# A tenth raw weight buffer, dead activation tiles as weight buffers in the last product, and one activation combination formed sooner

## The chip, the cores and the metric

The kernel runs on one core of a Trainium2 chip. The time is device microseconds (us) of one execution, from several timed runs; the profile is one further execution, taken by the hardware profiler. The core has five engines with a stream of instructions each: TensorE (PE in the profile: matmuls; PEld is its weight load), VectorE (DVE), ScalarE (ACT), GpSimd (POOL) and SyncE (SP). An engine takes its own instructions strictly in order; between engines there are semaphores. SP and POOL are used here mostly to issue transfers (DMAs) from the chip's HBM into the on-chip memory.

## The reference

The network has two layers and a final RMS norm, on 512 tokens of 1024 features, in float32.

```python
for l in range(DEPTH):                       # DEPTH = 2
    x = x + 0.5 * swiglu(rms_norm(x, ffn1_norm[l]), ffn1_w_in[l], ffn1_w_out[l])
    x = x + mixer(rms_norm(x, mix_norm[l]), mix_w_in[l], mix_gate_bias[l], na_rpb[l],
                  na_w_out[l], f_w_out[l], mix_w_o[l])
    x = x + 0.5 * swiglu(rms_norm(x, ffn2_norm[l]), ffn2_w_in[l], ffn2_w_out[l])
return rms_norm(x, final_norm)

def swiglu(x, w_in, w_out):                  # w_in 1024 x 5632, w_out 2816 x 1024
    g, u = jnp.split(x @ w_in, 2, axis=-1)
    return (jax.nn.silu(g) * u) @ w_out

# mixer: z = h @ w_in; neighbourhood attention on q, k, v; a 2-D DFT on uf; gates ga, gf
return (sigmoid(ga + gate_bias[0]) * y_na + sigmoid(gf + gate_bias[1]) * y_f) @ w_o
```

The mixer's `w_in` has 4096 columns, of which the last 2048 make the two gates. `w_o` is 1024 x 1024.

## The kernel before

**Arithmetic.** Each float32 operand of a large product is split into a high and a low part (ACT rounds the high part, DVE subtracts it from the value), and a product is three matmuls: high by high, high by low, low by high (lines 539, 540 and 542). Each large product is moreover formed by Strassen's scheme of seven block products instead of eight, numbered 1 to 7 by `m` in the code. A block product needs a combination of blocks of activations (`t5`, `t6`, `t7` for three of them in an FFN) and a combination of blocks of weights. The PSUM pairs A, B and C hold the seven results.

**Weights.** They are streamed from HBM in granules of 128 x 1024 float32 (512 KB), called `raw` when they land. For every granule there is a `Raw` object. Its `load` takes a buffer and issues the transfer on SP (line 155). Where `plus` is given, POOL then issues a second transfer that adds another granule onto the buffer as it lands, an accumulating DMA (line 165). DVE does other such sums itself (line 182). `Item.prep` then splits the granule: `whi` on ACT (line 210) and `wlo` on DVE (line 213). In the gates and in the output product one more accumulating DMA follows, from `Item.prep`, on POOL:

```python
            if self.then:
                G.dma_start(out=t, in_=wst[GRAN_AT[self.then]][:, 0:n], accum_op=ALU.add)   # line 215
```

The granule d that product 6 has just split gets block b added in place (`then=b.key`) and is split a second time for product 3. A block has two granules, so product 3 waits for two of these adds. They are issued after the splits for product 6, and POOL issues them in the place that the program gives them.

**Order.** One list of items runs through the whole program. `Stream.prep` issues loads ahead of the split, up to `depth` items beyond the one being split; `depth` is FETCH = 8 throughout. A load waits on SP until its buffer is free. In the FFNs, the gates and the mixer's output product the buffers are a ring of nine (`ffn_raw`, line 2022); in the rest of the mixer another ring (`mix_raw`). Since `load` issues the line 165 add right behind the SP load in the program, how far ahead the loads are issued also sets where those adds stand in POOL's program, against the line 215 adds.

**Stages.** Per layer: FFN1 (blocks of 2816 hidden columns, then the output product), mixer (attention, DFT, two gate blocks of seven products each, output product `w_o` on the pairs wA, wB, wC), FFN2, whose first block (`first_block`) runs while the norm of its input is still being finished. There DVE forms `t6` by the generator `combine`: a sum `xr` (line 651), a high part on ACT (line 656), and a low part `t6l` (line 658), behind product 5 in the code. The last output product of the network (`late`) runs with nothing behind it but the final norm.

Of the kernel before, what the change touches and what calls it, by code (L numbers as in the profile page):

```python
# [9 lines left out]
F32 = mybir.dt.float32  # L10
# [8 lines left out]
P = 128  # L19
# [15 lines left out]
FETCH = 8  # L35
# [63 lines left out]
def encoder_kernel(  # L99
# [15 lines left out]
    def nm(s):  # L115
        uid[0] += 1
        return f"{s}_{uid[0]}"

    def slot(dt=F32, s="k", shape=(4, 256)):
        return kp.tile([P, *shape], dt, tag="k", name=nm(s), bufs=23)  # L120
# [219 lines left out]
    ws = Stream()  # L340
    raw_pool = [None]
# [15 lines left out]
    def small(s, n=8):  # L357
        return sp.tile([P, 8], F32, tag=s, name=nm(s), bufs=2)[:, 0:n]
# [304 lines left out]
    def stage_ffn(norm, nxt, late):  # L663
# [45 lines left out]
        def combine(m):  # L709
            for _ in steps_of(m):  # L710
                pass
# [165 lines left out]
        def first_block():  # L877

            f0 = 2

            def snap_T(ps):
                t = slot(F32, "sn", (2, 256))
                S.activation(t, ps.rearrange("p (m t) -> p m t", m=2), AF.Copy)
                return t

            def less_T(ps, t):
                V.tensor_tensor(t, ps.rearrange("p (m t) -> p m t", m=2), t, ALU.subtract)

            pa, ha = pair("A"), bank("hA")
            product(pa, acts[1], K4, True)  # L890
            combine(5)
            s1 = snap(pa)
            if len(norm.due) == 2:
                norm.quad(*norm.due.pop(0))
            product_T(ha, acts[1], True)
            h1 = snap_T(ha)
            pb, hb = pair("B"), bank("hB")
            product(pb, acts[5], K4, True)
            combine(6)
            sb = snap(pb)  # L900
            norm.settle()
            product_T(hb, acts[5], True)
            hsb = snap_T(hb)
            norm.rstd()
            norm.spread(R)
            product(pa, acts[6], K4, False, again=True)
            s2 = snap(pa)
            combine(7)
            product_T(ha, acts[6], False)
            h2 = snap_T(ha)  # L910
            pc = pair("C")
            product(pc, acts[2], K4, True)
            less(pc, s1)
            combine(4)
            z1 = gate(s1, 0)
            product(pa, acts[7], K4, False, again=True)
            hc = bank("hC")
            product_T(hc, acts[2], True)
            less_T(hc, h1)
            r1 = half_gate(h1, 0)  # L920
            less(pa, sb)
            product_T(ha, acts[7], False)
            less_T(ha, hsb)
            product(pb, acts[3], K4, False, again=True)
            less(pb, s2)
            z2 = gate(s2, 1)
            times(z2, [sb[:, 0, :], sb[:, 1, :]], 1)
            product_T(hb, acts[3], False)
            less_T(hb, h2)
            r2 = half_gate(h2, 1)  # L930
            half_times(h2, r2, hsb, hsb, 1)
            z2 = words_apart(z2)
            product(pa, acts[4], K4, False, again=True)
            turned.append((turned_words(z2), 1, f0))
            times(z1, pa, 0)
            halves(z1, 0, f0)
            released(turned[-1][0])
            product_T(ha, acts[4], False)
            half_times(h1, r1, ha.rearrange("p (m t) -> p m t", m=2), h2, 0)
# [50 lines left out]

        if late or nxt.mix:
            tc.keep_in_program_order(S.activation(small("sq", 1), ones, AF.Sqrt))
        ps = {}
        for i, (m, c, _) in enumerate(steps):
            make(i)
# [135 lines left out]
    def stage_mixer(l, norm, nxt):  # L1131
# [783 lines left out]
        with tc.manual_schedule(engines={mybir.EngineType.DVE, mybir.EngineType.Activation}):  # L1915
            w = [ws.next(0), ws.next(0)]
            ws.prep(ws.pos + 1)
            ws.fetch(ws.prepped + 9)
            f_turn(0)
            h1 = high(t12, "t1")  # L1920
            acts[5] = low(h1, t12, "t1")
            for _ in fill(o, ns, 0, w):
                pass
            for z in B[1, 1]:
                V.tensor_tensor(t12, t12, z, ALU.add)
            h2 = high(t12, "t2")
            next(third)
            acts[6] = low(h2, t12, "t2")
            next(third)
# [89 lines left out]
    mix_pool = [None]  # L2019

    def ffn_raw(n):
        return scope_pool[0].tile([P, 1024], F32, tag="raw", name=nm("raw"), bufs=9)[:, 0:n]

    def mix_raw(n):
        return slot(F32, "raw", (1024,))

    scope_pool = [None]

    def swap_pools(kind, fetch=True):

        if scope[0]:
            scope[0].close()
        scope[0] = ExitStack()
        name = nm("stage")
        scope_pool[0] = scope[0].enter_context(tc.tile_pool(name=name, bufs=1, reuse_waits="tile"))
        if kind:
            mix_pool[0] = scope_pool[0]
            raw_pool[0] = mix_raw
        else:
            raw_pool[0] = ffn_raw  # L2040
        if fetch:
            ws.enter(ws.stage + 1)

# [207 lines left out]
```

## Time and profile before

| | |
|---|---|
| median of 3 runs | 1840.56 us (1840.37 to 1847.86) |
| the profiled execution's own time | 1838.69 us |
| its span, first to last instruction | 1836.9 us |
| mean granted TensorE clock | 0.999 |
| PE busy | 1824.8 us, 99% of the span |
| DVE busy | 1607.9 us, 88% |
| ACT busy | 1306.6 us, 71% |
| POOL busy | 179.2 us, 10% |
| transfers | 403.75 MB, mean 220 GB/s |

In the table of busy time, 99% for PE leaves little idle time to look for; the places where PE waits are in the view of waits. A row of that view reads: engine and line, what it waited for, microseconds in total, how many times, and the longest. In a timeline a row is start, duration, engine, line, operation, output<-inputs with shapes, count, and in square brackets the idle time of the engine before it with what released it. A row of the view of transfers tells the line of issue, the count, the size and the median us from issue to landing.

### The profile page before, as it was taken

What the parts mean: (1) busy time and instruction counts of PE and PEld (TensorE: products, weight loads), DVE (VectorE), ACT (ScalarE), POOL (GpSimd) and SP (SyncE); (2) the same over time, 40 slices, a digit from 0 to 9 for tenths busy, and PEclk for the clock granted to TensorE, in tenths of its full rate; (3) what the DMA queues carried; (4) which work ended last, traced back from release to release, by engine and by line L of the source; (5) the groups of instructions that cost most, each with busy time, mean ns of one, the idle gap of its engine ahead of it and who ended that gap; (6) DMA issues with size and microseconds to landing.
All of it is one profiled execution on the core that took longest, in us unless ns stands there. A gap on an engine that the chain in (4) does not pass through costs nothing.

```text
span 1836.9 us, 24500 instructions
## 1 busy us (share of the span) xinstructions
PE 1824.8 (99%) x8766; PEld 1509.6 (82%) x8766; DVE 1607.9 (88%) x1952; ACT 1306.6 (71%) x1771; POOL 179.2 (10%) x219
## 2 busy tenths in 40 slices
PE   9999999999999999999999999999999999999998
PEld 7888888887788888888888888888888788888886
DVE  7878899778889987889998888998789899887899
ACT  6777875767577776787666778766776776677865
POOL 0001011110111011001010100101001111100010
PEclk9999999999999999999999999999999999999999
DMA  9888798963997788879878887998649977988795
GB/s 303 222 236 224 187 277 267 227 175 112 276 240 186 170 228 234 217 199 281 249 188 215 232 217 196 263 305 184 177 135 262 234 184 184 236 214 223 199 290 143
DMA packets 206386, 403.75 MB, mean 220 GB/s; under 512 B 108732, under 2 KB 108892, under 8 KB 206264
## 3 DMA queue, kind: packets, MB, share of 16 engines
q1 hardware_dynamic: 176536, 300.52, 51.5%
q0 software_dynamic: 29296, 101.12, 30.2%
q8 instruction: 69, 1.13, 0.2%
q10 hardware_dynamic: 432, 0.55, 0.1%
q14 instruction: 53, 0.43, 0.1%
HBM read 370.67 MB, written 2.11 MB: 203 GB/s over the span
## 4 chain that ended last, share of the span: by engine, by line
PE 78%; DVE 7%; DMA 7%; issue 4%; ACT 3%; POOL 0%; SPq 0%; DVEq 0%; ACTq 0%; POOLq 0%
PE A L540 9%; PE A L542 9%; PE A L539 9%; DMA raw<-in_wst_dram 6%; PE o L542 6%; PE o L540 5%; PE o L539 5%; PE B L542 4%; PE B L540 4%; PE B L539 4%; DVE wlo L213 2%; PE ps L344 2%; PE C L542 2%; PE C L540 2%; PE C L539 2%
## 5 line engine op out<-in xcount | busy, mean ns | idle before, releaser
L213 DVE TENSOR_TENSOR wlo<-raw,whi 128x1024 fp32r<-128x1024 f32 (+1 forms) x534 | 632.0, 1193 | 164.6 <-ACT whi L210 163.0
L210 ACT ACTIVATE whi<-raw 128x1024 fp32r<-128x1024 f32 (+1 forms) x534 | 546.1, 1033 | 270.1 <-DVE raw L182 57.3
L165 POOL DMA_DIRECT2D raw<-in_wst_dram x170 | 148.7, 899 | 1301.9 <-DMA raw<-in_wst_dram 630.8
L182 DVE TENSOR_TENSOR raw<-raw,raw 128x1024 f32<-128x1024 f32 (+1 forms) x148 | 176.5, 1193 | 2.0
L540 PE MATMUL A<-whi,xl 128*128 128x512 f32 x400 | 155.8, 390 | 0.0
L539 PE MATMUL A<-whi,xh 128*128 128x512 f32 x400 | 155.8, 390 | 0.0
L394 ACT ACTIVATE at<-zt 128x1024 uint16<-128x1024 uint16 (+2 forms) x96 | 110.4, 1167 | 11.2 <-DMA zt<-zs 11.1
L205 ACT ACTIVATE whi<-raw 128x1024 fp32r<-128x1024 f32 (+1 forms) x83 | 85.7, 1037 | 43.4 <-PE A L540 13.3
L542 PE MATMUL A<-wlo,xh 128*128 128x512 f32 x400 | 115.1, 389 | 0.0
L206 DVE SCALAR_TENSOR_TENSOR wlo<-raw,whi 128x1024 fp32r<-128x1024 f32 (+1 forms) x83 | 98.7, 1195 | 11.5 <-ACT whi L205 11.5
L542 PEld LDWEIGHTS A<-wlo,xh 128*128 128x128 f32 x400 | 75.1, 188 | 15.5
L539 PEld LDWEIGHTS A<-whi,xh 128*128 128x128 f32 x400 | 75.1, 188 | 15.4
L540 PEld LDWEIGHTS A<-whi,xl 128*128 128x128 f32 x400 | 75.2, 188 | 15.4
L539 PE MATMUL B<-whi,xh 128*128 128x512 f32 x208 | 81.3, 391 | 0.8 <-ACT whi L210 0.8
L540 PE MATMUL B<-whi,xl 128*128 128x512 f32 x208 | 81.1, 390 | 0.0
L540 PE MATMUL C<-whi,xl 128*128 128x512 f32 x208 | 81.0, 390 | 0.0
L539 PE MATMUL C<-whi,xh 128*128 128x512 f32 x208 | 81.0, 390 | 0.0
L375 ACT ACTIVATE zs<-th 128x1024 uint16<-128x1024 uint16 x80 | 79.5, 1042 | 0.4 <-DVE th L801 0.4
L626 ACT ACTIVATE sn<-A 128x512 f32<-128x512 f32 x104 | 58.8, 586 | 27.3 <-PE A L542 27.2
L794 ACT ACTIVATE th<-sn,rh 128x512 f32<-128x512 f32 x80 | 54.9, 715 | 31.3 <-DVE sn L631 30.4
L542 PE MATMUL B<-wlo,xh 128*128 128x512 f32 x208 | 60.2, 391 | 0.2
L542 PE MATMUL C<-wlo,xh 128*128 128x512 f32 x208 | 60.1, 391 | 0.0
(451 smaller groups left out, 4624.2 us busy)
## 6 DMA issues: line engine op xcount, KB each, us to landing
raw<-in_wst_dram SPq DMA_DIRECT2D x468, 512.0 KB, 6.1
raw<-in_wst_dram POOLq DMA_DIRECT2D x180, 512.0 KB, 8.0
bm<-in_bias_dram SPq DMA_DIRECT2D x16, 512.0 KB, 5.5
raw<-in_wst_dram SPq DMA_DIRECT2D x30, 256.0 KB, 5.4
vs<-v SPq DMA_DIRECT2D x24, 128.0 KB, 5.4
x<-in_xin_dram SPq DMA_DIRECT2D x4, 512.0 KB, 10.2
raw<-in_wst_dram POOLq DMA_DIRECT2D x8, 256.0 KB, 8.2
dft<-in_dft_dram POOLq DMA_DIRECT2D x8, 256.0 KB, 6.8
```

Source lines behind the costliest of these rows:

```text
L165: G.dma_start(out=self.t, in_=wst[GRAN_AT[self.plus]][:, 0 : self.n], accum_op=ALU.add)
L182: V.tensor_tensor(self.raw.t, self.raw.t, self.add.t, ALU.add)
L205: S.activation(hi, t, AF.Copy, scale=-1.0)
L206: self.last = V.scalar_tensor_tensor(lo, t, -1.0, hi.bitcast(F32), ALU.mult, ALU.subtract)
L210: S.activation(hi[:, cs], t[:, cs], AF.Copy)
L213: self.last = V.tensor_tensor(lo[:, cs], t[:, cs], hi[:, cs].bitcast(F32), ALU.subtract)
L375: S.activation(s[:, h], words[:, h], AF.Copy)
L394: S.activation(to[:, w], t[:, w], AF.Copy)
L539: PE.matmul(ps, lh, rh, start=start, stop=False, skip_group_check=again)
L540: PE.matmul(ps, ll, rh, start=False, stop=False, skip_group_check=again)
L542: PE.matmul(ps, lh, rl, start=False, stop=stop, skip_group_check=again)
L626: last_snap[0] = S.activation(t[:, b, :], ps[b], AF.Copy)
```

## The change

Four edits.

1. The ring `ffn_raw` gets ten buffers instead of nine, and `depth` is FETCH + 1 = 9 wherever that ring is used (FFNs, gates, output product). At the start of the gates, `ws.fetch` goes to ten items instead of nine.
2. In the last FFN's output product the weights also go into the two buffers each of the tiles `xh` and `xl`, which no longer hold activations needed there: four further buffers of 1024 columns, then five from the ring. `depth` becomes 16.
3. In `first_block` (both FFN2s), the first step of combination 6 (`xr`, line 651) is taken by a hook after the first granule of product 5, and its other steps after the product.
4. `swap_pools` sets the depth back to FETCH in the parts of the mixer that use the other ring.

```diff
@@ first_block @@
-            product(pb, acts[5], K4, True)
-            combine(6)
+            six = steps_of(6)
+            product(pb, acts[5], K4, True, hook=lambda: next(six))
+            for _ in six:
+                pass
@@ stage_ffn, ahead of the output product @@
+        if late:
+            raw_pool[0] = late_raw
+            ws.depth = 16
@@ start of the gates @@
-            ws.fetch(ws.prepped + 9)
+            ws.fetch(ws.prepped + 10)
@@ the pools @@
-        return scope_pool[0].tile([P, 1024], F32, tag="raw", name=nm("raw"), bufs=9)[:, 0:n]
+        return scope_pool[0].tile([P, 1024], F32, tag="raw", name=nm("raw"), bufs=10)[:, 0:n]
+    spare = []
+
+    def late_raw(n):
+        if not spare:
+            for tag in ("xh", "xl"):
+                t = np_.tile([P, 2, 1024], F32, tag=tag, name=nm("raw"), bufs=2)
+                spare.extend(t[:, i, :] for i in range(2))
+            spare.extend([None] * 5)
+        t = spare.pop(0)
+        return ffn_raw(n) if t is None else t[:, 0:n]
@@ swap_pools @@
             raw_pool[0] = mix_raw
+            ws.depth = FETCH
         else:
             raw_pool[0] = ffn_raw
+            ws.depth = FETCH + 1
```

What this does to the order of instructions shows in three places.

The first is POOL at the first gate block of layer 0 (layer 1 is alike). `raw_4207` and `raw_4210` are the two granules of block d; their line 215 rows are the adds that product 3 waits for. The other rows are line 165 adds; `raw_4513` before and `raw_4497` after are the same granule, the first combined one of the second gate block. Before:

```order
L165 DMA raw_4207<-in_wst_dram 128x1024
L165 DMA raw_4210<-in_wst_dram 128x1024
L165 DMA raw_4279<-in_wst_dram 128x1024
L165 DMA raw_4282<-in_wst_dram 128x1024
L215 DMA raw_4207<-in_wst_dram 128x1024
L215 DMA raw_4210<-in_wst_dram 128x1024
L165 DMA raw_4513<-in_wst_dram 128x1024
L165 DMA raw_4556<-in_wst_dram 128x1024
```

After:

```order
L165 DMA raw_4207<-in_wst_dram 128x1024
L165 DMA raw_4210<-in_wst_dram 128x1024
L165 DMA raw_4275<-in_wst_dram 128x1024
L165 DMA raw_4282<-in_wst_dram 128x1024
L215 DMA raw_4207<-in_wst_dram 128x1024
L165 DMA raw_4497<-in_wst_dram 128x1024
L215 DMA raw_4210<-in_wst_dram 128x1024
L165 DMA raw_4516<-in_wst_dram 128x1024
```

The add for the next block now stands between the two line 215 adds.

The second is POOL at the mixer's output product of layer 0 (layer 1 is alike), where the line 215 rows belong to the output product's product 3 and the line 165 rows to FFN2 behind it. Before:

```order
L215 DMA raw_4880<-in_wst_dram 128x1024
L215 DMA raw_4901<-in_wst_dram 128x1024
L165 DMA raw_5264<-in_wst_dram 128x1024
L165 DMA raw_5288<-in_wst_dram 128x1024
L165 DMA raw_5342<-in_wst_dram 128x1024
```

After:

```order
L215 DMA raw_4864<-in_wst_dram 128x1024
L165 DMA raw_5260<-in_wst_dram 128x1024
L215 DMA raw_4883<-in_wst_dram 128x1024
L165 DMA raw_5267<-in_wst_dram 128x1024
L165 DMA raw_5291<-in_wst_dram 128x1024
```

Here too a line 165 add of the next stage comes between the two.

The third is DVE in FFN2's first block of layer 0 (layer 1 is alike): line 651 makes `xr`, line 658 `t6l`, lines 182 and 213 are weight sums and low parts, lines 365 to 367 small steps of the norm. Before:

```order
L182 TENSOR_TENSOR raw_5288<-raw_5288,raw_5223 128x1024
L367 SCALAR_TENSOR_TENSOR r_5644<-rt_5645,r_5644 128x4
L213 TENSOR_TENSOR wlo_5566<-raw_5264,whi_5565 128x1024
L365 TENSOR_TENSOR rt_5645<-r_5644 128x4
L651 TENSOR_TENSOR xr_5325<-xr_5490,xr_5325 128x1024
L366 SCALAR_TENSOR_TENSOR rt_5645<-rt_5645,ms_5641 128x4
L182 TENSOR_TENSOR raw_5342<-raw_5342,raw_5258 128x1024
L367 SCALAR_TENSOR_TENSOR r_5644<-rt_5645,r_5644 128x4
L658 TENSOR_TENSOR t6l_5584<-xr_5325,t6h_5583 128x1024
```

After:

```order
L651 TENSOR_TENSOR xr_5328<-xr_5493,xr_5328 128x1024
L367 SCALAR_TENSOR_TENSOR r_5644<-rt_5645,r_5644 128x4
L182 TENSOR_TENSOR raw_5267<-raw_5267,raw_5199 128x1024
L365 TENSOR_TENSOR rt_5645<-r_5644 128x4
L213 TENSOR_TENSOR wlo_5570<-raw_5260,whi_5569 128x1024
L366 SCALAR_TENSOR_TENSOR rt_5645<-rt_5645,ms_5641 128x4
L658 TENSOR_TENSOR t6l_5587<-xr_5328,t6h_5586 128x1024
```

The sum `xr` and the low part `t6l` each stand one large instruction earlier: two large ones (a line 182 and a line 213) stood between `xr`'s new place and its old one, and one line 182 sum that was ahead of `t6l` now comes behind it.

PE's order is the same before and after. SP issues the same loads, each about one granule earlier against the work.

## The prediction, made before the change was run

> **What bounds the kernel now.** I began with the page: busy time and the summary of the chain that ended last. Then I read PE's own waits, and a stretch in which nothing waits (the last row: window, length, busy time and count for PE, PEld, DVE, ACT and POOL, then the granted clock, the transfers' share and GB/s).
>
> ```profile
> PE 1824.8 (99%) x8766; PEld 1509.6 (82%) x8766; DVE 1607.9 (88%) x1952; ACT 1306.6 (71%) x1771; POOL 179.2 (10%) x219
> PE 78%; DVE 7%; DMA 7%; issue 4%; ACT 3%; POOL 0%; SPq 0%; DVEq 0%; ACTq 0%; POOLq 0%
> PE A L540 <- DVE t6l L658: 0.9, 2, 0.5
> PE B L539 <- ACT whi L210: 0.8, 1, 0.8
> PE o L542 <- DVE wlo L213: 0.2, 1, 0.2
> 500.00:550.00 50.00, 50.00 (x218) 40.42 (x218) 44.98 (x50) 36.10 (x38) 5.16 (x6) 1.00 0.92 238
> ```
>
> PE is busy for 1824.8 us, 12.1 short of the span of 1836.9 us. In the stretch from 500 to 550 us it does 218 matmuls without a gap, 0.229 us each, at a clock of 1.00; nothing can make these shorter here, since the change leaves PE's instructions and their order alone. So there are 12.1 us of idle PE time in all, and the three waits account for 1.9 us of them. A gain of over 0.5%, 9.2 us, isn't to be had. Losses have no such limit: PE has no slack to give, and any operand that comes later than now lengthens the run one for one. So the question is which operands come sooner and which come later.
>
> **The gains.** *Combination 6.* The row with `t6l` is the place that the third edit touches: PE wants it twice (once per FFN2) and waits 0.9 us in all, 0.5 at most.
>
> ```profile
> 614.69 1.22 DVE L182 TENSOR_TENSOR raw<-raw,raw 128x1024 f32<-128x1024 f32 x1
> ```
>
> In the changed order this large sum, 1.22 us, stands behind `t6l` and no longer ahead of it, which is more than either wait. So the waits go: 0.9 us (bounds nothing, if another operand is as late, and 2.4, the two sums). The sum that is moved back, and the low part that it feeds, are wanted by PE only a granule later.
>
> *Last output product.* Here the raw granules come late: ACT waits for them, and PE's weight load for what follows. The second part is for FFN1's output product of layer 1, which also gets one more buffer, the third for the rest of layer 1's gates.
>
> ```profile
> ACT whi L210 <- DMA raw<-in_wst_dram: 6.4, 4, 3.1
> PEld o L542 <- DVE wlo L213: 1.5, 3, 0.6
> PEld o L539 <- ACT whi L210: 0.4, 1, 0.4
> ...
> ACT whi L210 <- DMA raw<-in_wst_dram: 7.7, 5, 2.6
> PEld o L542 <- DVE wlo L213: 1.7, 4, 0.5
> ...
> PEld B L542 <- DVE wlo L213: 0.9, 2, 0.5
> ```
>
> (The views are the waits from 1765 to 1837 us, 1170 to 1225, and 1411 to 1460.) A weight load may wait in the shadow of a matmul still running, so its wait is the upper bound of PE's: 1.9 us for the last product, against 0.2 in PE's own list as the lower. With four more buffers and a depth of 16 its granules are asked for well ahead; I take 1.3 us, in the upper half, because the three waits there come one after another with nothing else late. For FFN1's product (0 to 1.7) one granule more of lead helps less against a queue already full: 0.5. For the gates (0 to 0.9): 0.5, as much from the PE delay told below as from the buffer. The four gains sum to 0.9 + 1.3 + 0.5 + 0.5 = 3.2 us.
>
> **The losses.** Ten buffers instead of nine let SP issue each load a granule sooner, and the line 165 add that belongs to a load moves up with it in POOL's program. At four places it moves between the two line 215 adds for which product 3 waits: the first gate block and the mixer's output product, in both layers. What an add costs that is queued behind another one, the trace shows at these very places. First POOL at the gates of layer 0, with its landing times (each of the three rows on transfers is the answer for one issue, in order: 483.87, 485.67, 487.41), then what waits:
>
> ```profile
> 483.87 0.85 POOL L215 DMA_DIRECT2D raw<-in_wst_dram  x1 [15.26 <-DVE wlo L213]
> 485.67 0.85 POOL L215 DMA_DIRECT2D raw<-in_wst_dram  x1 [0.95 <-DVE wlo L213]
> 487.41 0.86 POOL L165 DMA_DIRECT2D raw<-in_wst_dram  x1 [0.88 <-DMA raw<-in_wst_dram]
> 498.51 0.86 POOL L165 DMA_DIRECT2D raw<-in_wst_dram  x1 [10.24 <-DMA raw<-in_wst_dram]
> raw<-in_wst_dram POOLq DMA_DIRECT2D x1, 512.0 KB, 7.1
> raw<-in_wst_dram POOLq DMA_DIRECT2D x1, 512.0 KB, 11.1
> raw<-in_wst_dram POOLq DMA_DIRECT2D x1, 512.0 KB, 13.3
> 496.89 2.96 ACT L210 ACTIVATE whi<-raw 128x1024 fp32r<-128x1024 f32 x3 [3.79 <-DMA raw<-in_wst_dram]
> 498.00 0.50 PE L539 MATMUL B<-whi,xh 128*128 128x512 f32 x1 [0.78 <-ACT whi L210]
> ```
>
> The three are issued within 3.5 us and land at 491.0, 496.8 and 500.7: in the order of issue, the third 3.9 us behind the second. The second is the one that counts. ACT takes it up at 496.89, 0.1 us after it lands, and PE has already been waiting 0.78 us when it gets `whi`: slack zero. In the changed order this add is third, so it lands at about 500.7. POOL can issue it late by the wait of the add put ahead of it (0.88 us here) and 0.86 us for that issue, which still falls before the first one lands; the queue decides. Loss: **3.9 us**. Layer 1:
>
> ```profile
> 1397.20 0.85 POOL L215 DMA_DIRECT2D raw<-in_wst_dram  x1 [0.95 <-DVE wlo L213]
> 1399.99 0.86 POOL L165 DMA_DIRECT2D raw<-in_wst_dram  x1 [1.93 <-DMA raw<-in_wst_dram]
> raw<-in_wst_dram POOLq DMA_DIRECT2D x1, 512.0 KB, 10.2
> raw<-in_wst_dram POOLq DMA_DIRECT2D x1, 512.0 KB, 11.2
> 1407.49 2.96 ACT L210 ACTIVATE whi<-raw 128x1024 fp32r<-128x1024 f32 x3 [2.16 <-DMA raw<-in_wst_dram]
> 1408.60 0.19 PEld L539 LDWEIGHTS B<-whi,xh 128*128 128x128 f32 x1 [0.27 <-ACT whi L210]
> ```
>
> They land at 1407.4 and 1411.2; PE's weight load again waits already (0.27 us). Loss: **3.8 us**. For the output product, layer 0:
>
> ```profile
> 575.15 0.86 POOL L215 DMA_DIRECT2D raw<-in_wst_dram  x1 [20.91 <-ACT whi L210]
> 577.19 0.86 POOL L215 DMA_DIRECT2D raw<-in_wst_dram  x1 [1.18 <-DVE wlo L213]
> raw<-in_wst_dram POOLq DMA_DIRECT2D x1, 512.0 KB, 5.2
> raw<-in_wst_dram POOLq DMA_DIRECT2D x1, 512.0 KB, 8.3
> 585.60 1.06 ACT L210 ACTIVATE whi<-raw 128x1024 fp32r<-128x1024 f32 x1 [2.48 <-DMA raw<-in_wst_dram]
> 590.18 1.23 DVE L351 TENSOR_TENSOR m4l<-mq,m4h 128x1024 fp32r<-128x1024 f32 x1
> 591.83 0.39 PE L540 MATMUL wA<-whi,m4l 128*128 128x512 f32 x1
> ```
>
> Here the adds land at 580.4 and 585.5, 5.1 us apart. ACT takes the second up at 585.60, and the low part on DVE follows; behind that low part DVE's program has `mq`, then `m4l`, which ends at 591.41 and is read at 591.83. That is 0.4 us of slack; PE itself reads the granule's `whi` later than it is made, so the `m4l` chain binds. A third add in the queue puts the second 3.8 us later by the gate rows, 5.1 by the pair here; I take 3.8, as the third place in the queue is what was measured there. Loss: 3.8 - 0.4 = **3.4 us**. In layer 1 the same chain has 0.3 us of slack:
>
> ```profile
> 1501.37 1.23 DVE L351 TENSOR_TENSOR m4l<-mq,m4h 128x1024 fp32r<-128x1024 f32 x1
> 1502.92 0.39 PE L540 MATMUL wA<-whi,m4l 128*128 128x512 f32 x1
> ```
>
> Loss: **3.5 us**. The four sum to 3.9 + 3.8 + 3.4 + 3.5 = 14.6 us. Bounds for one place: nothing, if the queue lets the later add through unhindered, and 12.8 us, if POOL waits for the load of the add put ahead as it did at 498.51 (498.51 - 485.67), with the line 215 add behind it.
>
> The rest costs nothing that I can see. The load that the moved add needs is issued one granule sooner as well; elsewhere the earlier loads take SP and queue time that PE doesn't wait for. In the last product the extra buffers come free by PE's own reads of `xh` and `xl`.
>
> **A rule against the row.** The Trainium skill, "DMA: Bandwidth & Descriptors", section "Anatomy of one DMA — SWDGE (gpsimd) path", puts one GpSimd-issued DMA at a fixed 2.0 us plus bytes over 436 GB/s, most of the fixed part being completion latency; for 512 KB I estimate 1.2 us of movement, which is all that a queued DMA would add to the next. By that the four places would lose about 1.2, 1.2, 0.8 and 0.9, 4.1 us. The rows above have 3.8 to 5.1 us instead, while SP's queue is full too; I go by the rows.
>
> **The sum.** 14.6 - 3.2 = +11.4 us on the profiled execution's 1838.69 us: 1850.1. The median of the runs, 1840.56, is 1.9 us above that execution, so the runs should come to **1852.0 us**, 0.6% more than before. What can be told from no change is 0.5%, or 1831.4 to 1849.8 us.
>
> **The rivals.**
> *A. The moved adds are hidden.* POOL's transfers go through 16 engines side by side, and an add that is ready later might not hold up the next. Then only the gains stay: 1840.6 - 3.2 = 1837.4 us, no change by the bound. Against it: at the gates all three land in order, nearly evenly spaced, as in one queue. A cheap queued add belongs here too: a third of the spacing (1.3 us) at four places is 5.2 less 0.7 of slack, 4.5, and the time 1841.9. (The skill's figure would put it at about the same place: 4.1 - 3.2, so 1841.5.)
> *B. Only the gates pay.* At the output product the pair lands 5.2 and 8.3 us after issue, against 7.1 to 13.3 at the gates, so the queues are emptier there, and the add put between may land early enough. Then 7.7 - 3.2 = +4.5: 1845.1 us, no change by the bound. Against it: the second of that pair already lands 5.1 us behind the first.
> *C. POOL itself is blocked.* POOL waits in order for the load of the moved add, 10.24 us in one row above. If that happens at one of the four, with the line 215 add behind it, 12.8 us take the place of 3.8 there: 1852.0 + 9 = 1861.0. For it: the load comes through a queue whose transfers land late at the gates. Against it: the load is itself a granule earlier.
> *D. The gain is larger than PE's waits.* Only the 12.1 us of idle PE time could give it, and part of that is the start and the final norm. Faster by 0.5% would need nine of the twelve.
>
> **How the numbers follow.** I give the forecast 0.56, A 0.20, B 0.16, C 0.07, D 0.01. The forecast's own range is 1847 to 1857: with 2.6 us per place instead of 3.8 it is 4.8 less, with 5.1 it is 5.2 more. About four fifths of it lies above 1849.8, 0.46, which with C makes slower 0.53; same is 0.10 + 0.20 + 0.16 = 0.46; faster 0.01. For 8 in 10 the range reaches down to most of A and leaves the far end of C out: 1838 to 1857.
>
> **What would show it.** In the changed profile the waits of PE should have the row for `whi` behind product 3 of the gates at about 4 us, at both layers, and a wait of `wA` for `m4l` of 3 us or more at both output products. In POOL's timeline there, a line 165 add stands between the line 215 adds, and the second of these lands 3.8 us later than now against the first. The row for `t6l` should be gone, and the waits for `wlo` in the last output product with it. It is wrong if the second line 215 add lands no later than now (A), if POOL sits idle ahead of it for 10 us (C), or if `m4l` keeps its slack (B).

## The result

The changed kernel takes 1865.2 us (median of 5 runs, 1855.68 to 1871.07) against 1840.37 us before: a ratio of 1.013, with a 95% interval of 1.0091 to 1.017. Run again later beside other kernels it took 1869.72 us against 1839.19: 1.0155, 1.0135 to 1.0175. By the medians it is slower by 24.8 and 30.5 us, where the prediction had 11 us more and 1857 us at most. The profiled execution is the longest of the five, 1871.07 us with a span of 1869.3.

### The profile after

The page's table of busy time and PE's own waits:

```profile
PE 1830.0 (98%) x8766; PEld 1512.9 (81%) x8766; DVE 1608.3 (86%) x1952; ACT 1306.4 (70%) x1771; POOL 179.4 (10%) x219
PE o L539 <- ACT whi L210: 14.2, 1, 14.2
PE B L539 <- ACT whi L210: 10.9, 2, 6.2
PE wA L540 <- DVE m4l L351: 1.5, 2, 0.8
PE wB L539 <- ACT whi L210: 1.3, 2, 1.0
PE o L542 <- DVE wlo L213: 0.8, 2, 0.5
```

PE was idle for 12.1 us before and is for 39.3 now, and the 5.2 us more of busy time come from slower matmuls. The rows with B, wA and wB are the four places of the prediction, and the row for `t6l` is gone. The row with `o` is one wait of 14.2 us in the last output product, the place where a gain was forecast.

A view that adds things up by place helps here. For all 128 x 512 matmuls I took the distance from each one's start to the next one's and summed what is beyond 0.227 us, the usual distance, so that waits and slow matmuls both count. Lost PE time in us, from the traces:

| place | before | changed | difference |
|---|---|---|---|
| first gate block, layer 0 | 1.40 | 7.84 | +6.4 |
| first gate block, layer 1 | 0.52 | 7.29 | +6.8 |
| mixer's output product, layer 0 | 0.42 | 3.58 | +3.2 |
| mixer's output product, layer 1 | 0.41 | 2.85 | +2.4 |
| `t6`, both FFN2s | 1.42 | 0 | -1.4 |
| last output product | 1.28 | 16.55 | +15.3 |

These come to 32.7 us; the spans differ by 32.4. The first four come to 18.8 us here, and to 16.1 and 19.0 us in the two other profiles with this order of the adds (the changed kernel again, and without the late buffers). The last differs much more from run to run, as the experiments show.

**The first gate block, layer 0.** POOL's timeline, then the landing times of its first two issues, then two rows of the chain and PE's:

```profile
484.76 0.85 POOL L215 DMA_DIRECT2D raw<-in_wst_dram  x1 [15.07 <-DVE wlo L213]
489.16 0.85 POOL L165 DMA_DIRECT2D raw<-in_wst_dram  x1 [3.54 <-DMA raw<-in_wst_dram]
489.70 1.20 POOL L215 DMA_DIRECT2D raw<-in_wst_dram  x1
raw<-in_wst_dram POOLq DMA_DIRECT2D x1, 512.0 KB, 8.0
raw<-in_wst_dram POOLq DMA_DIRECT2D x1, 512.0 KB, 10.1
489.70 13.37 DMA raw<-in_wst_dram
503.18 1.07 ACT whi L210
504.29 0.80 PE L539 MATMUL B<-whi,xh 128*128 128x512 f32 x1 [6.17 <-ACT whi L210]
```

The line 165 add is between the two, POOL waited 3.54 us for its load, and the adds land at 492.7, 499.2 and 503.1. The last spacing is 3.8 us. PE's program is 0.9 us later here than before, so the second line 215 add is 5.4 us later against the work than its 496.8 was. Then comes what the prediction had no term for. The windows of the same trace (window, length, busy time with count for PE, PEld, DVE, ACT, POOL, granted clock, the transfers' share, GB/s):

```profile
498.00:500.00 2.00, 0.12 (x1) 0.00 (x0) 0.00 (x0) 0.00 (x0) 0.00 (x0) 1.00 1.02 258
500.00:502.00 2.00, 0.00 (x0) 0.00 (x0) 0.00 (x0) 0.00 (x0) 0.00 (x0) 0.59 1.07 287
504.00:506.00 2.00, 1.71 (x4) 1.43 (x5) 1.73 (x2) 2.00 (x3) 0.00 (x0) 0.50 0.27 61
506.00:508.00 2.00, 2.00 (x7) 1.56 (x7) 2.00 (x4) 0.13 (x1) 0.85 (x1) 0.71 0.70 240
595.00:605.00 10.00, 8.04 (x33) 5.43 (x32) 7.65 (x9) 7.94 (x15) 0.85 (x1) 1.00 0.92 247
505.31 0.63 PE L539 MATMUL B<-whi,xh 128*128 128x512 f32 x1
505.73 0.63 PE L540 MATMUL B<-whi,xl 128*128 128x512 f32 x1
```

The wait begins at 498.1 (504.29 less 6.17). By the share of 0.59 in the second row the granted clock falls to a half at 500.4, 2.2 us into the wait, and by the 0.71 in the fourth it is back at 507.2, 2.9 us after the work has come back: until then matmuls are 0.43 us apart instead of 0.23, and 1.5 us are lost on top. In layer 1 the clock falls 2.6 us into the wait and is back 4.7 us after the work, and 2.4 us are lost. In the output products, where no single wait is over 1.2 us, the clock stays at 1.00 (fifth row). The Trainium skill has this rule, "TensorE: Matmul & The Clock Gate", Part 1: after an idle window of about 3.4 us the array is clocked at half, and comes back after about as long a stretch of work; the four times here agree with it within 1.3 us.

**The last output product.** POOL's timeline and the landing times of its two issues; two rows on the waits, of the chain and of ACT; then all transfers in 2.5 us, first of the kernel before at its last transposing DMAs (from 1727.5 us), then of the changed one (from 1755.5):

```profile
1750.98 0.87 POOL L165 DMA_DIRECT2D raw<-in_wst_dram  x1 [6.85 <-DVE at L814]
1753.97 0.87 POOL L165 DMA_DIRECT2D raw<-in_wst_dram  x1 [2.12 <-DMA raw<-in_wst_dram]
raw<-in_wst_dram POOLq DMA_DIRECT2D x1, 512.0 KB, 21.7
raw<-in_wst_dram POOLq DMA_DIRECT2D x1, 256.0 KB, 21.1
1750.80 21.59 DMA zt<-zs
ACT at L394 <- DMA zt<-zs: 16.9, 1, 16.9
```

```profile
DMA packets 2108, 0.62 MB, mean 250 GB/s; under 512 B 2083, under 2 KB 2083, under 8 KB 2108
q1 hardware_dynamic: 2108, 0.62, 116.2%
```

```profile
DMA packets 256, 0.11 MB, mean 43 GB/s; under 512 B 245, under 2 KB 245, under 8 KB 256
q1 hardware_dynamic: 243, 0.06, 91.4%
q0 software_dynamic: 13, 0.05, 13.9%
```

`zt<-zs` is a transfer of another kind: SP sends the activations of a finished block through the DMA engines to be transposed, in packets of 256 bytes. ACT takes its result up (line 394), and `whi` stands behind that in ACT's program: so PE's wait bears the name of a weight that had long landed (at 1753.4 us). Before, 2108 packets go through in 2.5 us. In the changed kernel, with POOL's two adds under way and SP's next loads just issued, 256 do, at 43 GB/s, and the engines are busy all the same (105%). The transposing DMA is done 21.6 us after its issue, the adds after 21.7 and 21.1.

### The profile page after: what moved, and what is told of

Its sections match the earlier page's. It is cut to its first block, busy times and chain, and to the rows that moved or that the text cites. A ratio compares the mean times of both kernels' runs of the same rounds, so it can differ in the third digit from the quotient of the medians.

```text
span 1869.3 us, 24500 instructions
## 1 busy us (share of the span) xinstructions
PE 1830.0 (98%) x8766; PEld 1512.9 (81%) x8766; DVE 1608.3 (86%) x1952; ACT 1306.4 (70%) x1771; POOL 179.4 (10%) x219
## 4 chain that ended last, share of the span: by engine, by line
PE 79%; DMA 8%; DVE 7%; ACT 3%; issue 2%; POOL 0%; SPq 0%; DVEq 0%; ACTq 0%; POOLq 0%
PE A L539 9%; PE A L540 9%; PE A L542 9%; DMA raw<-in_wst_dram 6%; PE B L539 5%; PE B L542 5%; PE B L540 5%; PE o L542 5%; PE o L539 5%; PE o L540 5%; PE C L539 2%; PE C L540 2%; PE C L542 2%; PE ps L344 2%; PE ps L345 2%
## 5 line engine op out<-in xcount | busy, mean ns | idle before, releaser
L540 PEld LDWEIGHTS A<-whi,xl 128*128 128x128 f32 x400 | 75.1, 188 | 15.4
L539 PEld LDWEIGHTS A<-whi,xh 128*128 128x128 f32 x400 | 75.1, 188 | 15.4
```

What stands on the lines that cost most here:

```text
L539: PE.matmul(ps, lh, rh, start=start, stop=False, skip_group_check=again)
L540: PE.matmul(ps, ll, rh, start=False, stop=False, skip_group_check=again)
```

## The experiments

Each comparison is with the kernel before on the same chip. "Adds" are POOL's accumulating DMAs. The ratio and its interval are the comparison's own, not the quotient of the two medians; where an event comes only in some executions the two differ. Each run has one profile, of one of its executions, and what a profile shows need not hold for the others.

### Without the late buffers

```diff
-        if late:
-            raw_pool[0] = late_raw
-            ws.depth = 16
```

> The changed kernel without the second edit (no extra buffers and no depth of 16 in the last output product); all else as changed. Theory: the loss has two separate parts, the moved line 165 adds at the gates and the output products of both layers (+18.8 us in the profile after: 7.84 and 7.29 us of lost PE time at the gates against 1.40 and 0.52 before, 3.58 and 2.85 at the output products against 0.42 and 0.41), and one stall in the last output product (+15.3), which comes from the second edit. Then about 1840 + 18.8 - 1.4 (t6) = 1857 us here, and the 14 us wait of o for whi is gone. Rival: the stall in the last product comes from the earlier loads of the first edit; then it stays, and the time is about 1866 to 1871.

1858.35 us against 1841.57; ratio 1.0084, 1.0059 to 1.0109. The profile has no wait in the last output product over 0.5 us. The gates and output products lose 8.2, 7.4, 3.4 and 2.8 us, as in the changed kernel. But one new place stands in B's row, the second gate block of layer 0 with 8.9 us, which in the changed kernel's first profile lost 0.6:

```profile
PE B L539 <- ACT whi L210: 16.4, 4, 5.8
```

So the loss at the four places doesn't need the second edit, and the last product's stall is not in this profile without it. There is also a third place that can stall.

### The late buffers and `t6` alone

The ring stays at nine and the depth at 8; the second and third edits are as in the change.

> The kernel before with the second and third edits alone (late buffers with depth 16, t6 sooner); the ring stays at nine and the depth at 8. Theory: the gates and output products of the mixer are as before, t6 gains 1.4 us, and the last output product has the stall in some form: 1840 - 1.4 + up to 15, so 1841 to 1854 us, with ACT waiting for zt over 10 us in the profile. Rival, that the second edit does what it was costed at (its weights come sooner, 1.3 us gained): 1838 us and no wait for zt there.

1838.78 us against 1841.57; ratio 0.9986, 0.9965 to 1.0006, no change that can be told. The stall in the last product is not there (0.99 us lost), nor is the loss at the four places, so the rival was nearer: the second edit alone does no harm that can be told, and the four places need the first. The trace suggests why the stall is missing. Here too SP sends a burst of nine loads right behind the last transposing DMA, from 1739.4 to 1744.2:

```profile
1740.12 0.86 POOL L165 DMA_DIRECT2D raw<-in_wst_dram  x1 [8.77 <-DVE wlo L213]
1744.16 0.86 POOL L165 DMA_DIRECT2D raw<-in_wst_dram  x1 [3.17 <-DVE wlo L213]
```

The packets of the transposing DMA run from 1738.7 to 1741.9. POOL's next two adds are issued behind its first packet, and their own packets begin at 1744.4, when it is through. In the changed kernel, with a granule more of lead, the first of the two adds is issued 1.3 us ahead of the first packet (1750.98 and 1752.3). A burst of loads is therefore not enough. The second gate block lost 6.4 us in this profile; its first add, issued at 523.29 beside a transposing DMA, took 13.1 us to land (second of the rows below), where the same add took 7.8 before (third):

```profile
PE B L539 <- ACT whi L210: 4.4, 2, 3.7
raw<-in_wst_dram POOLq DMA_DIRECT2D x1, 512.0 KB, 13.1
```

```profile
raw<-in_wst_dram POOLq DMA_DIRECT2D x1, 512.0 KB, 7.8
```

### The old order of the adds

All edits, but the next block's add is held behind the second line 215 add at the four places:

```diff
-                G.dma_start(out=t, in_=wst[GRAN_AT[self.then]][:, 0:n], accum_op=ALU.add)
+                gate = G.dma_start(out=t, in_=wst[GRAN_AT[self.then]][:, 0:n], accum_op=ALU.add)
+                after = behind_then.get(self.raw.key)
+                if after:
+                    waiting, held[after] = held[after], gate.ins
+                    with tc.issue_after(gate.ins):
+                        for raw in waiting:
+                            raw.summed()
...
+    for l_ in range(L):
+        behind_then[(l_, 0), "gd", 0, 1] = (l_, 0), "gd", 1, 0
+        behind_then[(l_, 0), "wd", 0, 1] = (l_, 2), "d", 0, 0
+    held.update({key: [] for key in behind_then.values()})
```

> The changed kernel with one thing put back: at the gates and at the mixer's output product, both layers, the line 165 add for the next block is held behind the second line 215 add on POOL, as before. Ten buffers, depths and SP's order stay. Theory (queue order on POOL): the stalls at the four places go back to before's 0.4 to 1.4 us, 18.8 us less than the changed kernel in the same condition: 1839 us plus whatever the last product costs (0 to 15), so 1840 to 1854. Rival (the tenth buffer itself crowds the transfers at the gates, wherever the adds stand): the stalls of 5 and 6 us at the gates stay, 1860 us and more.

Median 1849.74 us against 1841.57, executions from 1839.06 to 1859.66; ratio 1.0023, 0.9991 to 1.0055. The first gate blocks lose under 0.5 us each, the output products 0.41 each. All 18.8 us are back. What is left is chiefly the last output product (14.9 us in this profile), with 2.7 and 1.2 us at the second gate blocks of the two layers. That the slower ones of the other executions have the same stall is likely and not shown. PE's waits:

```profile
PE o L550 <- ACT whi L210: 12.6, 1, 12.6
PE B L550 <- ACT whi L210: 2.4, 3, 1.3
```

### Only the order, in the kernel before

The kernel before, with the add of the next gate block put between the two line 215 adds (L220 and L168 in its own numbering), and nothing else:

```diff
+                if self.raw.key in late_then:     # ((l, 0), "gd", 0, 1), both layers
+                    deferred.append(add_then)
+                else:
+                    add_then()
...
+                        while deferred:           # in Raw.load, behind self.summed()
+                            with tc.issue_after(first.ins):
+                                deferred.pop(0)()
```

> The kernel before with only the order on POOL changed, at the first gate block of both layers: the add for the next block goes between the two line 215 adds. Ring of nine, depth 8, all other edits left out. Theory: the second add lands one place later in the queue, 3.8 us, and PE, once it has stood still for some 4 to 5 us, comes back at about half its clock for some us, as in the changed profile (matmuls 0.43 us apart instead of 0.23 from 1423.9 to 1428.5 us): 2 x (3.8 + 2) = 11.6, about 1852 us. As predicted, without the clock: 1848. Rival (a moved add is harmless, the tenth buffer does it): 1840.

1851.74 us against 1841.57; ratio 1.0046, 1.0025 to 1.0067. The first gate blocks lose 7.2 and 8.4 us, against 1.4 and 0.5 before: +13.7 by the order alone, with nine buffers, where the changed kernel has +13.2.

```profile
PE B L551 <- ACT whi L213: 10.7, 3, 5.8
484.25 0.85 POOL L220 DMA_DIRECT2D raw<-in_wst_dram  x1 [14.14 <-DVE wlo L216]
487.26 0.85 POOL L168 DMA_DIRECT2D raw<-in_wst_dram  x1 [2.17 <-DMA raw<-in_wst_dram]
487.80 1.20 POOL L220 DMA_DIRECT2D raw<-in_wst_dram  x1
```

The three land at 491.7, 497.4 and 501.2: again 3.8 us between the last two. The median fits the account with the clock (1852) better than the one without (1848), but the interval, 1846 to 1854, holds both. The profile decides: the granted clock falls to a half at both waits, which costs 2.3 and 2.5 us there.

### The old order and no late buffers, twice

> Tenth buffer with its depths and t6 sooner, the adds on POOL held in the old order at the four places, and no late buffers (first and third edits without what hurt). Theory: all that the changed kernel lost is the moved adds and the last output product's stall, so this is the kernel before less t6's 1.4 us and some of the small waits: about 2 us under before. Rival: the tenth buffer costs something of its own, then over before by some us.

1834.32 us against 1839.19; ratio 0.9972, 0.995 to 0.9995. The same kernel again:

> The kernel that was 0.28% under before (interval 0.05 to 0.5), again, with more rounds: the tenth buffer, t6 sooner, old order of the adds, no late buffers. If the gain holds: ratio 0.996 to 0.999. If it was chance: 0.999 to 1.001.

1843.17 us against 1839.63, from 1832.9 to 1853.72; ratio 1.0002, 0.998 to 1.0024. The gain did not hold up. Its profile has a wait of 3.7 us in the last output product, with a transposing DMA beside an add that took 15.2 us to land. So with ten buffers the stall can come there, in a smaller size, even without the late buffers.

### The adds held behind the transposing DMA

The old order at the four places, all edits, and two of the last output product's adds wait for the last transposing DMA, by the means that the kernel has for its first FFN blocks (`released`):

```diff
+        out_sums = [(stage, "oc", 0, g) for g in range(2)] if late else []
+        held.update({key: [] for key in out_sums})
...
+            if jb == NB - 1 and late:
+                released(turned[-1][0], out_sums)
```

> The kernel with the order restored at the four places and all edits in (median 1849.7 when it ran, 1839 to 1860, with a stall of 12.8 us in the profile while the transposing DMAs zt<-zs and two accumulating DMAs were under way together), with one more thing held: the last output product's adds wait on POOL until the last transposing DMA has landed. The burst of eight SP loads behind it stays. Theory (accumulating DMAs beside a transposing one make both crawl): the stall is gone, the last transposing DMA lands within 3 to 5 us of issue, and the time is 2 to 3 us under before, with little spread. Rival (the burst of loads, from the depth of 16, crowds the transposing DMA out): the stall of 10 us or more stays, median about 8 us over before.

1838.3 us against 1839.19, from 1833.92 to 1849.3; ratio 1.0004, 0.9983 to 1.0025. In the profile the stall is gone (0.64 us lost in the last product) with the burst of loads still there, which speaks for the adds and against the burst:

```profile
1729.58 3.01 SPq L392 DMA_TRANSPOSE zt<-zs  x1
1732.68 17.39 SPq L155 DMA_DIRECT2D raw<-in_wst_dram  x13
1736.10 0.53 POOL L768 DMA_DIRECT2D seen<-zt  x1 [13.04 <-DMA zt<-zs]
1736.68 1.77 POOL L165 DMA_DIRECT2D raw<-in_wst_dram  x2
```

But the profiled execution is the fastest of ten. The little spread that was expected didn't come: it is 15.4 us, against 20.6 with the old order alone, on another chip. The same hold in the kernel with nine buffers:

> The second and third edits with a ring of nine (1838.8, 2.8 us under before when it ran) and the same hold of the last output product's adds behind the last transposing DMA. Theory: there the adds came behind the transposing DMA by themselves, so the hold changes nothing: 2 to 4 us under before. If the hold costs time (adds that land later than PE wants them), it shows as waits for whi in the last output product, 1 us or more.

1837.66 us against 1839.19; ratio 0.9993, 0.9983 to 1.0003, 1.11 us lost in the last product: no price worth naming, no gain that can be told.

### One of the kernel's own holds taken out

This starts from the kernel with the old order and no late buffers:

```diff
-        late_sums = [(stage, "c", 1, g) for g in range(2)]
+        late_sums = []
```

> The best kernel so far (tenth buffer, t6 sooner, old order of the adds at the four places, no late buffers; 1834.3 when it ran) without one wait that the kernel before already has: in the first block of three FFNs two line 165 adds wait on POOL for a transposing DMA zt<-zs to land. Here they are issued ahead of that wait, beside the transposing DMA. No extra loads, no deep queue. Theory (adds beside a transposing DMA make both crawl): stalls of some us at one or more of the three places, 3 to 20 us over the kernel it was made from, and adds there that take over 12 us to land. Rival (the last output product's stall was a matter of that place's many loads alone): within 2 us of it.

1835.82 us against 1839.63; ratio 0.999, 0.9967 to 1.0013. The profile has no stall at the three places: at each an add was under way beside a transposing DMA, issued 5.8 to 7.5 us ahead of its first packet, and that DMA took 2.4 to 3.7 us. The theory's stalls there didn't come; a meeting needn't be costly. But six executions lie at 1833 to 1837 and four at 1846 to 1851, and the profiled one, the longest, lost 14.7 us in one wait, at the second gate block, and 2.6 more through the clock. Its add there took 23.9 us:

```profile
PE B L550 <- ACT whi L210: 14.6, 1, 14.6
522.97 0.86 POOL L215 DMA_DIRECT2D raw<-in_wst_dram  x1 [15.10 <-DVE wlo L213]
raw<-in_wst_dram POOLq DMA_DIRECT2D x1, 512.0 KB, 23.9
```

### Four adds held

Now also the two adds ahead of those, which lay beside the transposing DMA before the last (`for q in "dc"` in `out_sums`).

> All edits with the old order at the four places, and all four of the last output product's first adds (before, two of the four) held on POOL until the last transposing DMA has landed. Theory: the spread that was left with two adds held (1834 to 1849 in ten executions) came from the other two, beside the transposing DMA before the last; then the times draw together at about 1834 to 1836, unless the two now come too late for PE (a wait for whi of 1 to 5 us, the same in every execution). Rival: the spread has another place, such as the second gate block, where before too has slower executions; then it stays.

1834.41 us against 1839.63, five executions from 1833.07 to 1836.39; ratio 0.9962, 0.9948 to 0.9976. Again, with more executions:

> All edits, old order at the four places, and the last output product's first four adds behind the last transposing DMA, again with more rounds (1834.4, ratio 0.9948 to 0.9976, in five executions). If both causes are named rightly and removed, the median stays 3 to 6 us under before; single executions may still be some us slower by the second gate block, where line 215 adds and a transposing DMA still meet (that DMA took 9.6 and 22 us in the profiles of two kernels, where the adds lay beside it, against 2 to 4 as a rule). If the five were luck: ratio 0.999 to 1.001.

1839.01 us against 1842.8, from 1834.99 to 1854.18; ratio 0.999, 0.9968 to 1.0012. The narrow spread of the five executions had been luck; in this profile the second gate block lost 2.9 us and its transposing DMA took 7.4.

### The second gate block's adds held too

Its two line 215 adds, both layers, wait for the second transposing DMA there:

```diff
+                behind = self.raw.key[1:3] == ("gd", 1)
+                with tc.issue_after(then_gate[0]) if behind else nullcontext():
...
+                then_gate[0] = G.dma_start(out=to, in_=turned[j][0:1, 0, 0, 0:32].bitcast(F32)).ins
```

> The same with one more hold: the second gate block's two line 215 adds, both layers, wait on POOL for the second transposing DMA there. Theory (adds beside a transposing DMA are what makes executions differ): no execution is over 4 us above the fastest, each transposing DMA takes under 5 us, but the adds start 4 to 6 us later than now and were wanted within 1 us of landing, so each layer waits about 3 to 5 us there and, if PE stands still for 4 us, loses up to 2.5 us more at half its clock: 6 to 14 us over the kernel without this hold, in every execution. Rival (the second gate block's slow executions come from the loads around it): the spread stays.

1846.7 us against 1842.8; ratio 1.0022, 1.001 to 1.0035. All twelve executions lie between 1843.43 and 1848.69, a spread of 5.3 us where 4 had been expected at most, against 19.2 without this hold in the same session. No transposing DMA takes over 4.5 us. PE still waits at the two places, now for adds that start later: 6.0 and 8.7 us lost. Over the kernel without the hold the median is 7.7 us more, inside the forecast of 6 to 14:

```profile
PE B L552 <- ACT whi L210: 9.7, 2, 5.6
```

### The transposing DMA moved away

The adds stay; the transposing DMA goes behind product 6, and the output product's first two adds, wanted much later, wait for it:

```diff
-            1, bias, acts, {1: lambda: taken(1), 5: lambda: taken(0), 2: lambda: channels(1), 7: lambda: channels(0)}
+            1, bias, acts, {1: lambda: taken(1), 2: lambda: channels(1), 6: lambda: taken(0), 3: lambda: channels(0)}
```

> All edits, old order at the four places, the last output product's first four adds behind the last transposing DMA, and in the second gate block no hold of the line 215 adds: instead the second transposing DMA is issued behind product 6 instead of behind product 5 (its words are joined behind product 3 instead of 7), and the mixer output product's first two adds, which PE wants some 25 us later, wait on POOL for it. Theory: no add is under way beside a transposing DMA at either place and nothing is wanted early, so no execution is over 4 us above the fastest and the median is 5 us or more under before, ratio 0.995 to 0.998. If the later transposing DMA meets the line 215 adds still landing, the spread stays; if the words come too late for the output product, a wait of wA at its start of 1 us or more, in every execution.

1834.09 us against 1840.89, eight executions from 1833.22 to 1835.68; ratio 0.9956, 0.994 to 0.9973. No transposing DMA takes over 4.3 us. PE's longest wait, beyond the start, is 0.7 us:

```profile
PE B L551 <- ACT whi L210: 0.7, 1, 0.7
523.34 0.86 POOL L215 DMA_DIRECT2D raw<-in_wst_dram  x1 [15.67 <-DVE wlo L213]
525.07 0.86 POOL L215 DMA_DIRECT2D raw<-in_wst_dram  x1 [0.88 <-DVE wlo L213]
539.17 0.53 POOL L1978 DMA_DIRECT2D seen<-zt  x1 [13.24 <-DMA zt<-zs]
539.69 0.92 POOL L165 DMA_DIRECT2D raw<-in_wst_dram  x1
```

Both stalls and the spread are gone together in these eight executions, without a price that shows. This version is faster than the kernel before, by 0.27 to 0.6% (the ends of the interval). The adds at the last product take up to 20 us to land here, with no transposing DMA beside them: six are issued within 8 us and land one after another, 2.6 to 3.8 us apart. A long landing alone is therefore no sign of a meeting.

### The changed kernel again

> The changed kernel itself again, beside the others on one chip. Both accounts of the loss expect 13 us at the gates and 5 to 6 at the output products in any execution (their waits are set by the order of the queue), and a last output product whose stall differs from execution to execution (0 to 15 us): about 24 us over before, times spread over 15 us.

1869.72 us against 1839.19, four executions from 1865.18 to 1876.72. In its profile the two first gate blocks lose 7.0 and 5.7 us, the output products 3.3 and 2.8, the last product 18.5, the second gate block 8.0.

## Why the prediction was wrong

**The direction and the place were right.** "At four places it moves between the two line 215 adds": so it did, and these four places lose 18.8 us more than before in the profile, where 14.6 were forecast. The old order alone takes them away; the new order alone, in the kernel before, brings the gates' part. The queue's term held at the gates: the second line 215 add lands 3.8 and 3.9 us behind the one put ahead of it, and the same in the kernel with the order alone. At the output products it is 2.8 and 3.0 us. The 1.2 us for a queued add, which the prediction estimated from the Trainium skill, "DMA: Bandwidth & Descriptors", section "Anatomy of one DMA — SWDGE (gpsimd) path", doesn't hold here. Rivals A and B are out.

**The output products** were put at 3.4 and 3.5 us, and lose 3.2 and 2.4. The second line 215 add lands 8.6 and 7.8 us behind the first, against 5.1 and 4.5 before, so it is 3.5 and 3.3 us later. The wait for `m4l` is the last one there, as described, but it is 0.8 us each time and not the 3 us or more that was named as the sign: PE waits ahead of it for `whi` of the late granule (1.0 us in layer 0), `wlo` and `m4h`, which the prediction took to have time to spare.

**The gates** were put at 7.7 and lose 13.2 more than before. Two terms were mis-sized. "POOL can issue it late by the wait of the add put ahead of it (0.88 us here) [...] the queue decides": that wait was 3.54 us in layer 0, so the second line 215 add went out 4.0 us later than before, and the queue decides only from there: 5.4 us later against the work instead of 3.9. This is rival C in small. And these long waits have a second price that the sum left out, the clock: 1.5 us in layer 0 and 2.4 us in layer 1. So "any operand that comes later than now lengthens the run one for one" puts it too low. The forecast itself made waits of 4.7 us (0.78 and 3.9) and 4.1 us (0.27 and 3.8). What follows for the clock is stated by the Trainium skill, "TensorE: Matmul & The Clock Gate", Part 1, and I didn't weigh it.

**The last output product** is the step that failed: "With four more buffers and a depth of 16 its granules are asked for well ahead; I take 1.3 us". A gain of 1.3 us was forecast and 15.3 us were lost in the profile. The loads do come sooner. But so do their adds, and "The rest costs nothing that I can see" put nothing for that. With the first edit's lead two of them are issued beside the last transposing DMA; both crawl, and the product stands still for up to 16 us. I counted what the step issues and asked which queue it is moved past on POOL; I didn't ask what SP's queue is doing at that time that is no load. The kernel's own text has a hold that keeps adds behind a transposing DMA in the first FFN blocks; it shows in the waits of the kernel before, and would have been the hint:

```profile
POOL seen L754 <- DMA zt<-zs: 62.6, 3, 23.4
```

**The `t6` term** held: 1.4 us gained by the distances of starts, 0.9 by the waits. The small gains in FFN1 and in the later gates can't be told from the spread.

What is shown, and what isn't: that the meeting of adds and a transposing DMA makes these stalls is shown by taking it away in three ways (adds held at the last product, adds held at the second gate block, the transposing DMA moved). Each left SP's loads as they were, and in each of the profiles the transposing DMA at that place took 4.5 us or less; with the adds held at the second gate block PE then waits for the held adds instead. Why a DMA engine does so little while busy stays open. Why some meetings do no harm is open too, but the time of issue matters, as the last section shows. It doesn't settle every case: the adds at the second gate block meet the transposing DMA in the kernel before as well, one of them issued 1.5 us ahead of its first packet, and there it lands in 7.8 us.

## What to carry to other kernels

More buffers and more lead move everything that a load brings with it, in every queue that it goes through: look at what stands next to each moved transfer afterwards, also in the other queue. On a critical add, count its place in the queue and the waits of whatever is put ahead of it on the issuing engine. In the sixteen profiles every wait of PE of 3.7 us or more had the clock at a half at its end or behind it and lost 1.5 to 2.9 us more by that, and no wait of up to 1.3 us did (the first 20 us left aside). Waits in between don't occur, so where it sets in is not shown.

## What the runs showed that I had not expected

A transposing DMA of 512 KB beside accumulating DMAs can take 22.1 us instead of 2 to 4, and the adds crawl with it. Counting its 2048 packets of 256 bytes from the first to the last (46 such DMAs in a run): in the kernel before the median is 2.6 us and the longest takes 4.1. In the changed kernel's two profiles the last one takes 17.7 and 19.5 us, and at the second gate block one takes 22.1 us in the kernel without one of the kernel's own holds, 13.4 without the late buffers, and 9.6 with the late buffers and nine buffers. Every one over 5 us in sixteen profiles, 19 of 736, has an add under way beside it that was issued 0.9 to 2.7 us ahead of its first packet; the adds beside them took 8 to 25 us to land. An add was issued 0.5 to 3 us ahead of the first packet 71 times in all, and the other 52 of these DMAs took 4.9 us at most. The 665 DMAs without such an add took 4.6 us at most, also where an add was issued earlier, or only behind the first packet. So in these traces the long ones need an add issued shortly ahead, and that alone is not enough. This is a count; no run varied the time of issue alone.

The kernel before may get its spread from this too, in part at least: 1838.0 to 1848.1 us in twelve executions, against 1833.2 to 1835.7 in the eight beside them where the two were kept apart at both places. That is argued and not shown: the two kernels differ in more than this, and the one profile of the kernel before has no long transposing DMA.
